# One decoder layer on one core: the causal mask moved into VectorE's maximum, compressed keys stored by residue modulo 8, and a rewritten order of steps

## The chip, the core and the metric

The kernel runs on one core of one Trainium2 chip. The core has five engines that run side by side: TensorE (PE in the rows; PEld is its weight load), VectorE (DVE), ScalarE (ACT), GpSimd (POOL) and SyncE (SP), which here only issues DMA transfers. The metric is the device time of one execution in microseconds, lower being better; a time is the median of three runs.

## The reference, cut to what matters

One layer of a decoder works on 512 tokens of width 1024. A modulated normalisation feeds one input projection, whose columns feed two groups of heads; their outputs are concatenated and projected, and a gated MLP with a short convolution follows. The change touches the sparse attention of eight query heads with two groups of keys:

```python
q = rope_partial(rmsnorm(to_heads(q_pre, NSA_HEADS, hd), q_g), pos)
k_c = rope_partial(rmsnorm(to_heads(kc_pre, G, hd), k_g[0]), pos)
...
cidx = np.arange(n_cmp)[:, None] * 16 + np.arange(32)[None]        # 31 overlapping blocks of 32 tokens
flat = (k_c[:, :, cidx] + pe).reshape(B, G, n_cmp, 32 * 64)
k_cmp = silu(flat @ w1) @ w2                                       # the same for v_cmp
...
sc = jnp.where(kpos <= t, q @ k.T * scale, NEG)                    # selected and window branch
p = softmax(sc); o = p @ v
```

With 512 tokens the selected branch keeps all of its eight blocks and the window covers all earlier tokens, so that both branches are causal attention over all earlier keys, with keys and values of their own.

## The kernel before

All tokens lie in four tiles of 128. The program has three stages. First the modulation's first columns, the normalised input and the projections of the queries and of one gate are worked out (to about 57 us). Then comes a stage in which everything else of the first sub-layer is interleaved by hand (to about 275 us). Then the output projection, the up-projection and the down-projection follow; they are long rows of matmuls with 512 columns.

Products of float32 quality are made from two rounded parts each (`split`, lines 139 to 141: ScalarE makes the high part, VectorE the rest; `mm3`, lines 143 to 146: three matmuls). Weights come through two buffers `raw`: `take` issues the load of the next weights when the present ones are taken, `piece` splits a half of them one use ahead. SyncE issues all loads in program order, each when its buffer has been read.

The middle stage is seven Python generators. The strings of `ORDER` say, letter by letter, which one emits its next step; each engine executes its instructions in the order in which they are emitted and waits only for data and buffers. In this document d46 is the step of the 47th letter `d`, counted from 0.

- `d`: dense work. d0 to d15 are the projection of keys and values, d16 to d23 the projection for the compressed branch, d24 to d39 two projections of the recurrent heads, d40 is `cmp_flat` (it forms the blocks with their position sums), and `cmp_hidden` multiplies them by `w_cmp1` in four quarters: d46, d48, d58 and d60 hold the matmuls (line 888). d53 to d56 and d61 to d64 project values; d65 to d72 project and turn others, the first turning being emitted in d69 and the second in d73 (line 1253).
- `p`: squares, roots, rope (`norm`, lines 689 to 704) and turning of queries, keys and compressed inputs.
- `a`: attention. A unit is a tile, a head and one or two branches: tiles 0 and 1 take both branches in one unit (16 units), tiles 2 and 3 one branch (32 units). An even `a` step emits the scores and their maximum, the following odd one the exponential.
- `c`: `cmp_out` in four steps; c0 applies the activation to what d60 has summed, c1 turns it, c2 multiplies by `w_cmp2`.
- `s`: sums of the modulation on VectorE (line 1333), one load of 512 KB each.
- `l`, `m`: levels of the recurrence of two pairs of heads.

For the mask, units of tiles 0 and 1 add it on TensorE, by a matmul of an identity with the mask (line 981), and VectorE takes one maximum over both branches (line 982); the exponential reads PSUM. Units of tiles 2 and 3 do it in one VectorE instruction that adds the mask, takes the maximum and writes the masked scores to SBUF (line 978).

For the compressed branch, a tile's keys and values are written twice side by side for each group, turned by four transposes (line 838), and copied so that even tokens lie in the lower 64 partitions and odd ones in the upper (lines 841, 842). d40 adds the positions in eight instructions that read every eighth element, four on VectorE and four on GpSimd (line 875).

Of the kernel before, what the change touches and what calls it, by code (L numbers as in the profile page):

```python
# [19 lines left out]
P = 128  # L20
# [35 lines left out]
ORDER = ("pddpddpppspddppddsdppspdpddpddpppddpsdpdddddpdpddpdpdddddppaspddaapaddaspapsaddaddsdalpppapaadlddlld",  # L56
         "aadadadsladasaladlldaadlddallladdddslaalllddsaaalddcddcsamcllmcdaaamlaadaaldmsadaadamaaaaamamsdlaala",
         "daadlammdalmaadmamaldsaaadmmmlaammaadlmmlasmdalaaaaamadaadaaddasadamdmmsadmllalaaaasmmammaalmaadamsl",
         "aadldddmmaasasldaadaaamlaaadmmladmaaaasamamdaaaamldds")
# [40 lines left out]
def hybrid_layer_kernel(ctx: ExitStack, tc: tile.TileContext, d: dict, out: bass.AP, dbg=None):  # L100
# [353 lines left out]
    identb = cst.tile([P, P], BF16, name="identb")  # L454
    causb = cst.tile([P, P], BF16, name="causb")
# [6 lines left out]
    def gate_tables():  # L462
        gp.tensor_copy(identb, ident)
# [225 lines left out]
    def norm(n):  # L689
# [5 lines left out]
        for hf in range(2):  # L695
            ve.tensor_tensor(rt[:, :, :, 8 * hf:8 * hf + 8], xr[:, :, :, 8 - 8 * hf:16 - 8 * hf],
                             st[:, :, 8 * hf:8 * hf + 8].unsqueeze(2).to_broadcast([P, t, g, 8]), ALU.mult)
# [6 lines left out]
        n.append(dst)  # L704

    def prep(steps):

        for step in steps:
            for f, u in [(w[0], w[1:]) for w in step.split()]:
                if f == "s":  # L710
                    units[u] = squares(makers[u[0]](int(u[1])))
                elif f == "r":
                    root(units[u])
                elif f == "n":
                    norm(units[u])
                elif f == "f":
                    units[u][0][4](units[u])
                else:
                    units[u][0][5](units.pop(u))
            yield  # L720
# [5 lines left out]
    def hg_forget(pr, j, a):  # L726
# [8 lines left out]
        ve.tensor_scalar(k[:, :, ::1 - 2 * j], t3, fc2n[:, h:h + 1], fc2[:, h:h + 1], ALU.mult, ALU.add)  # L735

    def hg_query(pr, j, a):
# [4 lines left out]
        ve.scalar_tensor_tensor(HG[pr][2][:, j], th, 1.0, a, ALU.add, ALU.mult)  # L742

# [63 lines left out]
    kv2 = G([2, 2, 256], s="kv2")  # L807
# [14 lines left out]
    def a_unit(i):  # L822
        def copy_vg(n):
# [3 lines left out]
            vd = TMP([P, 2, 2, HD], tag="vd")  # L827
            sc.copy(vd, acca[i][:, P:2 * P].rearrange("p (g e) -> p g e", e=HD).unsqueeze(2)
                    .to_broadcast([P, 2, 2, HD]))
            n.append(vd)  # L830

        def flip_kv(n):
            ps = PS()
            for b in range(2):
                for g in range(2):
                    q = b * 2 + g
                    src = n[3][:, g] if b else n[2][:, 0, g]
                    pe.transpose(ps[:, q * P:(q + 1) * P], src.rearrange("p a e -> p (a e)"), ident)
            pv = ps.rearrange("p (q u two) -> p q u two", q=4, two=2)
            kv = kv2.rearrange("p b g u -> p (b g) u")  # L840
            sc.copy(kv[0:64, :, i * 64:(i + 1) * 64], pv[0:64, :, :, 0])
            sc.copy(kv[64:128, :, i * 64:(i + 1) * 64], pv[64:128, :, :, 1])

        return (acca[i][:, 0:P].rearrange("p (a g e) -> p a g e", a=1, e=HD), stab[:, i:i + 1, 1],
                ctab[:, i:i + 1, 1], 2, copy_vg, flip_kv)
# [19 lines left out]
    def cmp_flat():  # L865
        ps = PS()
        pe.transpose(ps[:, 0:32], perow, ident[0:32, 0:32])
        ve.tensor_copy(pet, ps[:, 0:32])
        for b in range(2):
            f = G([16, 2, 32], s="flat")  # L870
            gp.memset(f[:, :, :, 31:32], 0.0)
            for g in range(2):
                for m2 in range(2):
                    src = kv2[:, b, g, 8 * m2:8 * m2 + 248].rearrange("p (n m) -> p m n", m=8)
                    (gp if g else ve).tensor_tensor(f[:, 8 * m2:8 * m2 + 8, g, 0:31], src,
                                                    pet[:, b * 16 + 8 * m2:b * 16 + 8 * m2 + 8].unsqueeze(2)
                                                    .to_broadcast([P, 8, 31]), ALU.add)
# [4 lines left out]
    def cmp_hidden(mq):  # L882
        w1 = take(f"w1{mq}")
        yield
        for m in range(4):
            for b in range(2):
                mm = 4 * mq + m
                pe.matmul(cps[0][64 * b:64 * b + 64, 0:256], FL[b][:, mm].rearrange("p g n -> p (g n)"),
                          w1[:, b, m], start=(mm == 0), stop=(mm == 15))
        yield  # L890

    def cmp_out():
        cth = TMP([P, 256], tag="cth")
# [26 lines left out]
        for g in range(2):  # L920
            ve.tensor_tensor(BD[:, g], ps[:, 64 + g * HD:64 + (g + 1) * HD].unsqueeze(1).to_broadcast([P, 4, HD]),
                             cb[:, C_BLK:C_BLK + 4].unsqueeze(2).to_broadcast([P, 4, HD]), ALU.mult)
        yield
# [17 lines left out]
    def cmp_scores(i):  # L941
        ps = PS("S")
# [22 lines left out]
    def scores(u):  # L965
        i, h, bs = u
        if h is None:
            return cmp_scores(i)
        g, W, n = h // 4, (i + 1) * P, len(bs)
# [4 lines left out]
        pe.matmul(o, QS[i][:, h], KK[g, 1][:, 0:i + 1, bsl], start=False, stop=(n == 1))  # L974
        mx = SM([P, 2], "mx")
        if n == 1:
            pt = TMP([P, 512], tag="pt")
            ve.tensor_tensor_reduce(pt[:, 0:W], ps[:, 0:W], cmask[:, 512 - W:512], -1.0, 1e30, ALU.add, ALU.min,
                                    mx[:, 0:1])
            return pt, mx  # L980
        pe.matmul(o[:, i], identb, causb.unsqueeze(1).to_broadcast([P, n, P]), start=False, stop=True)
        ve.tensor_reduce(mx[:, 0:n], ps[:, 0:n * W].rearrange("p (b w) -> p b w", b=n), AX.X, ALU.max,
                         negate=True)
        return ps, mx

    def expo(u, st):
# [4 lines left out]
        ps, mx = st  # L991
        W, n = (i + 1) * P, len(bs)
        pt = ps if n == 1 else TMP([P, 512], tag="pt")
# [3 lines left out]
        for e in range(n):  # L997
            sl = slice(e * W, (e + 1) * W)
            sc.activation(pt[:, sl], ps[:, sl], AF.Exp, bias=mx[:, e:e + 1], scale=(-1.0 if n == 1 else 1.0),
# [736 lines left out]
```

## Time and profile before

| what | value |
|---|---|
| median of three runs | 699.4 us (698.62 to 699.52) |
| the profiled execution | 699.39 us |
| its span, from first to last instruction | 697.6 us |
| busy share of PE, DVE, ACT, POOL | 98%, 65%, 47%, 17% |
| granted clock of TensorE | full in all 40 slices |

The profile comes from one execution, whose own time is that of the median; 1.8 us of it lie outside the span. Busy time of TensorE is modelled with a tail that overlaps the next matmul, so it is better to read the starts of its instructions: the distance between two starts is what an instruction costs when nothing waits.

### The profile page before, as it was taken

The page shows a single profiled execution, that of the slowest core. Times are in us where ns is not written, and L with a number is a line of the kernel's source. Part 1 is how long each engine was busy: PE and PEld are TensorE (multiplying, and loading weights), DVE is VectorE, ACT ScalarE, POOL GpSimd, SP SyncE. Part 2 cuts the span into 40 slices and gives each one's busy share as a digit, 9 for nine tenths or more (in the row PEclk, how much of TensorE's full clock was granted, in tenths as well). Part 3 has the DMA queues.
Part 4 walks back from the last instruction along what each step waited for, and adds up shares of the span by engine and source line. Part 5 has one row for each costly group of instructions (what it writes and reads, how often), then busy time and mean ns, then how long its engine had stood idle before and what let it go on. Part 6 is the DMA issues. An engine that isn't in the chain of part 4 may idle for free.

```text
span 697.6 us, 10902 instructions
## 1 busy us (share of the span) xinstructions
PE 687.0 (98%) x4263; PEld 566.5 (81%) x4264; DVE 453.2 (65%) x882; ACT 326.0 (47%) x624; POOL 117.5 (17%) x119
## 2 busy tenths in 40 slices
PE   8999999999999999999999999999999999999997
PEld 4678898787887879888988888888888888888886
DVE  5588989968889879688656666655555554225224
ACT  5564446665676778245444443344433443111210
POOL 2005022200020200100047437511011010000000
PEclk9999999999999999999999999999999999999999
DMA  9996443568213226162053454523424323124301
GB/s 284 295 291 196 124 148 97 187 205 272 92 33 121 62 62 214 59 178 69 12 163 117 132 152 122 150 71 110 121 61 120 96 86 122 62 101 170 120 31 60
DMA packets 100487, 90.16 MB, mean 129 GB/s; under 512 B 5787, under 2 KB 83539, under 8 KB 100437
## 3 DMA queue, kind: packets, MB, share of 16 engines
q1 hardware_dynamic: 100181, 89.38, 42.0%
q8 instruction: 33, 0.54, 0.3%
q10 hardware_dynamic: 256, 0.11, 0.1%
q14 instruction: 17, 0.14, 0.1%
HBM read 87.37 MB, written 2.11 MB: 128 GB/s over the span
## 4 chain that ended last, share of the span: by engine, by line
PE 77%; DVE 10%; ACT 5%; DMA 4%; SPq 2%; issue 1%; POOL 0%; ACTq 0%; DVEq 0%
PE u L146 11%; PE u L144 11%; PE u L145 11%; PE dn L144 6%; PE dn L145 6%; PE dn L146 6%; PE pT L144 2%; PE pT L146 2%; PE pT L145 2%; PE oT L1059 2%; PE F L1031 2%; PE oh L144 2%; PE oh L146 2%; PE oh L145 2%; DMA raw<-in_w_in 1%; DVE rows L399 1%
## 5 line engine op out<-in xcount | busy, mean ns | idle before, releaser
L141 DVE TENSOR_TENSOR wlo<-raw,whi 128x1024 fp32r<-128x1024 f32 (+1 forms) x87 | 111.3, 1280 | 136.1 <-ACT whi L140 135.5
L140 ACT CAST whi<-raw 128x1024 fp32r<-128x1024 f32 (+1 forms) x87 | 89.8, 1032 | 102.3 <-PE dn L146 80.1
L144 PE MATMUL u<-h2h,whi 128*128 128x512 f32 (+1 forms) x360 | 136.7, 380 | 0.0
L145 PE MATMUL u<-h2l,whi 128*128 128x512 f32 (+1 forms) x360 | 136.7, 380 | 0.0
L146 PE MATMUL u<-h2h,wlo 128*128 128x512 f32 (+1 forms) x360 | 136.6, 380 | 0.0
L145 PEld LDWEIGHTS u<-h2l,whi 128*128 128x128 f32 x360 | 67.7, 188 | 12.9
L146 PEld LDWEIGHTS u<-h2h,wlo 128*128 128x128 f32 x360 | 67.7, 188 | 12.8
L144 PEld LDWEIGHTS u<-h2h,whi 128*128 128x128 f32 x360 | 67.7, 188 | 12.7
L145 PE MATMUL dn<-wlo,gT 128*128 128x512 f32 (+1 forms) x160 | 62.1, 388 | 0.0
L146 PE MATMUL dn<-whi,gT 128*128 128x512 f32 (+1 forms) x160 | 62.1, 388 | 0.0
L144 PE MATMUL dn<-whi,gT 128*128 128x512 f32 (+1 forms) x160 | 62.0, 388 | 0.0
L1623 POOL TENSOR_TENSOR y<-y,y 128x512 f32<-128x512 f32 x22 | 28.4, 1290 | 165.7 <-DVE y L1618 165.7
L140 ACT CAST gT<-y 128x512 fp32r<-128x512 f32 x20 | 12.4, 622 | 71.2 <-POOL y L1623 71.2
L141 DVE TENSOR_TENSOR gT<-y,gT 128x512 fp32r<-128x512 f32 x20 | 14.8, 742 | 42.7 <-ACT gT L140 42.7
L144 PE MATMUL pT<-hT,whi 128*128 128x512 f32 x96 | 39.2, 409 | 0.0
L146 PE MATMUL pT<-hT,wlo 128*128 128x512 f32 x96 | 37.7, 393 | 0.0
L145 PE MATMUL pT<-hT,whi 128*128 128x512 f32 x96 | 37.5, 391 | 0.0
L1621 ACT ACTIVATE y<-y 128x512 f32<-128x512 f32 x22 | 13.9, 632 | 49.6 <-DVE y L1618 49.6
L145 PEld LDWEIGHTS dn<-wlo,gT 128*128 128x128 f32 x160 | 30.0, 188 | 6.4 <-DVE wlo L141 0.2
L144 PEld LDWEIGHTS dn<-whi,gT 128*128 128x128 f32 x160 | 30.0, 188 | 6.2
L146 PEld LDWEIGHTS dn<-whi,gT 128*128 128x128 f32 x160 | 30.0, 188 | 6.2
L1616 ACT ACTIVATE y<-u,cv 128x512 f32<-128x512 f32 x44 | 33.9, 772 | 0.0
(378 smaller groups left out, 1410.2 us busy)
## 6 DMA issues: line engine op xcount, KB each, us to landing
raw<-in_w_up SPq DMA_DIRECT2D x44, 512.0 KB, 4.2
aw<-in_w_ada SPq DMA_DIRECT2D x24, 512.0 KB, 4.0
raw<-in_w_down SPq DMA_DIRECT2D x10, 1024.0 KB, 5.1
ada<-in_w_ada SPq DMA_DIRECT2D x32, 256.0 KB, 5.7
raw<-in_w_in SPq DMA_DIRECT2D x7, 1024.0 KB, 6.6
x<-in_x SPq DMA_DIRECT2D x8, 512.0 KB, 4.8
raw<-in_w_cmp SPq DMA_DIRECT2D x8, 512.0 KB, 5.6
raw<-in_w_out SPq DMA_DIRECT2D x4, 1024.0 KB, 6.1
```

Of the source, the lines that this page charges most:

```text
L140: sc.copy(hi, src)
L141: (eng or ve).tensor_tensor(lo, src, f32(hi), ALU.subtract)
L144: pe.matmul(o, ah, bh, start=start, stop=False, skip_group_check=True)
L145: pe.matmul(o, ah, bl, start=False, stop=False, skip_group_check=True)
L146: pe.matmul(o, al, bh, start=False, stop=stop, skip_group_check=True)
L399: ve.scalar_tensor_tensor(t, w, cs[:, j:j + 1], t, ALU.mult, ALU.add)
L1031: pe.transpose(ps[:, j * P:(j + 1) * P], src[:, j * P:(j + 1) * P], ident)
L1059: pe.matmul(oTs[i][r:r + 64, h // 2], VV[:, j, b, g], src[:, q * P:(q + 1) * P], start=(h == 0 and b == 0 and j == 0), stop=False, skip_gr ...
L1616: sc.activation(y, u, AF.Identity, bias=cv[:, 132 + c:133 + c], scale=cv[:, 88 + c:89 + c])
L1621: sc.activation(y, y, AF.Silu)
L1623: gp.tensor_tensor(ys[0], ys[0], y, ALU.mult)
```

## The change

- The mask of tiles 0 and 1 is added as in tiles 2 and 3: one VectorE instruction for each branch adds it, takes the maximum and writes to SBUF. The mask matmul, its two constant tiles and the maximum over both branches go.
- Compressed keys and values are no longer doubled: two transposes for a tile instead of four, and four smaller copies instead of two, which sort the tokens by their residue modulo 8. The position sums read neighbouring elements, in four VectorE instructions over both groups; GpSimd takes no part.
- The rope's product of swapped halves is one instruction for each tile and projection, with the halves read in reversed order, instead of two.
- `ORDER` has the same 353 letters, with the same count of each, in another sequence.

The lines that only add to a set `there` or assert on it while the program is built are left out.

```diff
-ORDER = ("pddpddpppspddppddsdppspdpddpddpppddpsdpdddddpdpddpdpdddddppaspddaapaddaspapsaddaddsdalpppapaadlddlld",
-         "aadadadsladasaladlldaadlddallladdddslaalllddsaaalddcddcsamcllmcdaaamlaadaaldmsadaadamaaaaamamsdlaala",
-         "daadlammdalmaadmamaldsaaadmmmlaammaadlmmlasmdalaaaaamadaadaaddasadamdmmsadmllalaaaasmmammaalmaadamsl",
-         "aadldddmmaasasldaadaaamlaaadmmladmaaaasamamdaaaamldds")
+ORDER = ("dppddpsdppddppppdppdddpsdsdppdpdpdpddpsddpddddpddpddpdddppadpsddaapdaappaapdsddsdddaapapadaaddsdddaa",
+         "dsldaallaallaadllaapdlldsdddddladlasldslddlaalldcmcaacalascdddmllaaaalamddldaaaadmaasamaaamlamsdaama",
+         "ddaaladmlammamsdmaalmalmdadaamlamamamadaadaasllaammasdadadsaaaalmasdamadlamadaamldaammlasmlmadaammma",
+         "mlalddddlmsaalasmaadamaaadaaadlaasmaaasmdddaamaaadlma")
...
         rt = TMP([P, t, g, 16], tag="rt")
-        for hf in range(2):
-            ve.tensor_tensor(rt[:, :, :, 8 * hf:8 * hf + 8], xr[:, :, :, 8 - 8 * hf:16 - 8 * hf],
-                             st[:, :, 8 * hf:8 * hf + 8].unsqueeze(2).to_broadcast([P, t, g, 8]), ALU.mult)
+        for a in range(t):
+            ve.tensor_tensor(rt[:, a].rearrange("p g (two e) -> p g two e", two=2),
+                             xr[:, a, :, 0:16].rearrange("p g (two e) -> p g two e", two=2)[:, :, ::-1],
+                             st[:, a].rearrange("p (two e) -> p two e", two=2).unsqueeze(1)
+                             .to_broadcast([P, g, 2, 8]), ALU.mult)
...
-    kv2 = G([2, 2, 256], s="kv2")
+    kv2 = G([2, 2, 8, 32], s="kv2")
...
-            vd = TMP([P, 2, 2, HD], tag="vd")
-            sc.copy(vd, acca[i][:, P:2 * P].rearrange("p (g e) -> p g e", e=HD).unsqueeze(2)
-                    .to_broadcast([P, 2, 2, HD]))
+            vd = TMP([P, P], tag="vd")
+            sc.copy(vd, acca[i][:, P:2 * P])
...
-            for b in range(2):
-                for g in range(2):
-                    q = b * 2 + g
-                    src = n[3][:, g] if b else n[2][:, 0, g]
-                    pe.transpose(ps[:, q * P:(q + 1) * P], src.rearrange("p a e -> p (a e)"), ident)
-            pv = ps.rearrange("p (q u two) -> p q u two", q=4, two=2)
-            kv = kv2.rearrange("p b g u -> p (b g) u")
-            sc.copy(kv[0:64, :, i * 64:(i + 1) * 64], pv[0:64, :, :, 0])
-            sc.copy(kv[64:128, :, i * 64:(i + 1) * 64], pv[64:128, :, :, 1])
+            for b, src in enumerate((n[2].rearrange("p t g a e -> p (t g a e)"), n[3])):
+                pe.transpose(ps[:, b * P:(b + 1) * P], src, ident)
+            pv = ps[:, 0:256].rearrange("p (b u two) -> p b u two", b=2, two=2)
+            for g in range(2):
+                for r in range(2):
+                    sc.copy(kv2[64 * r:64 * r + 64, :, g, :, 8 * i:8 * i + 8],
+                            pv[64 * g:64 * g + 64, :, :, r].rearrange("p b (n m) -> p b m n", m=8))
...
-                ctab[:, i:i + 1, 1], 2, copy_vg, flip_kv)
+                ctab[:, i:i + 1, 1], 1, copy_vg, flip_kv)
...
-            for g in range(2):
-                for m2 in range(2):
-                    src = kv2[:, b, g, 8 * m2:8 * m2 + 248].rearrange("p (n m) -> p m n", m=8)
-                    (gp if g else ve).tensor_tensor(f[:, 8 * m2:8 * m2 + 8, g, 0:31], src,
-                                                    pet[:, b * 16 + 8 * m2:b * 16 + 8 * m2 + 8].unsqueeze(2)
-                                                    .to_broadcast([P, 8, 31]), ALU.add)
+            for m2 in range(2):
+                ve.tensor_tensor(f[:, 8 * m2:8 * m2 + 8, :, 0:31],
+                                 kv2[:, b, :, :, m2:m2 + 31].rearrange("p g m n -> p m g n"),
+                                 pet[:, b * 16 + 8 * m2:b * 16 + 8 * m2 + 8].unsqueeze(2).unsqueeze(3)
+                                 .to_broadcast([P, 8, 2, 31]), ALU.add)
...
-        pe.matmul(o, QS[i][:, h], KK[g, 1][:, 0:i + 1, bsl], start=False, stop=(n == 1))
+        pe.matmul(o, QS[i][:, h], KK[g, 1][:, 0:i + 1, bsl], start=False, stop=True)
         mx = SM([P, 2], "mx")
-        if n == 1:
-            pt = TMP([P, 512], tag="pt")
-            ve.tensor_tensor_reduce(pt[:, 0:W], ps[:, 0:W], cmask[:, 512 - W:512], -1.0, 1e30, ALU.add, ALU.min,
-                                    mx[:, 0:1])
-            return pt, mx
-        pe.matmul(o[:, i], identb, causb.unsqueeze(1).to_broadcast([P, n, P]), start=False, stop=True)
-        ve.tensor_reduce(mx[:, 0:n], ps[:, 0:n * W].rearrange("p (b w) -> p b w", b=n), AX.X, ALU.max,
-                         negate=True)
-        return ps, mx
+        pt = TMP([P, 512], tag="pt")
+        for e in range(n):
+            ve.tensor_tensor_reduce(pt[:, e * W:(e + 1) * W], ps[:, e * W:(e + 1) * W], cmask[:, 512 - W:512], -1.0,
+                                    1e30, ALU.add, ALU.min, mx[:, e:e + 1])
+        return pt, mx
...
-            sc.activation(pt[:, sl], ps[:, sl], AF.Exp, bias=mx[:, e:e + 1], scale=(-1.0 if n == 1 else 1.0),
+            sc.activation(pt[:, sl], pt[:, sl], AF.Exp, bias=mx[:, e:e + 1], scale=-1.0,
```

## Rows read from the trace of the kernel before

**Rows 1.** The page's line of busy time, share of the span and instructions of each engine.

```profile
PE 687.0 (98%) x4263; PEld 566.5 (81%) x4264; DVE 453.2 (65%) x882; ACT 326.0 (47%) x624; POOL 117.5 (17%) x119
```

**Rows 2.** Busy time in three stretches: the interleaved stage, ten microseconds within it, and the up-projection. Columns: stretch, its length, then busy time and instructions of PE, PEld, DVE, ACT and POOL, the granted clock, the DMA engines' share, GB/s.

```profile
57.00:275.00 218.00, 215.43 (x1983) 180.08 (x1982) 186.65 (x468) 139.61 (x341) 30.75 (x44) 1.00 0.43 138
...
125.00:135.00 10.00, 10.00 (x118) 8.20 (x120) 9.83 (x18) 5.69 (x18) 4.17 (x5) 1.00 0.35 124
...
340.00:570.00 230.00, 230.00 (x1056) 192.16 (x1055) 132.53 (x151) 99.22 (x134) 73.07 (x54) 1.00 0.39 114
```

**Rows 3.** TensorE's instructions in order of time, at a mask matmul (L981) and at the transposes of compressed values (L838). Columns: start, duration, engine, line, operation, tiles, shape, count.

```profile
133.69 0.28 PE L981 MATMUL S<-causb,identb 128*128 128x256 bf16 x1
133.81 0.38 PE L1031 MATMUL F<-cb,pt 128*128 128x128 f32 x2
...
125.97 0.38 PE L838 MATMUL ps<-cb,vd 128*128 128x128 f32 x2
126.19 0.38 PE L1031 MATMUL F<-cb,pt 128*128 128x128 f32 x2
```

**Rows 4.** TensorE's groups of instructions by line and shape in the interleaved stage: count, busy us, mean ns of one, idle time before them.

```profile
L981 PE MATMUL S<-causb,identb 128*128 128x256 bf16 x16 | 4.5, 283 | 0.0
...
L838 PE MATMUL ps<-cb,dst 128*128 128x128 f32 x8 | 1.6, 280 | 0.0
...
L838 PE MATMUL ps<-cb,vd 128*128 128x128 f32 x8 | 1.5, 273 | 0.0
```

**Rows 5.** TensorE's instructions in order of time, the four of the interleaved stage with the longest idle time before them; the idle time and what ended it stand in brackets.

```profile
81.96 0.66 PE L751 MATMUL ps<-cb,dst 128*128 128x128 f32 x4 [0.48 <-DVE dst L702]
...
163.06 1.94 PE L888 MATMUL cps<-raw,flat 128*64 128x256 f32 x14 [0.41 <-DMA raw<-in_w_cmp]
...
207.26 0.65 PE L1253 MATMUL ps<-cb,hvT 128*128 128x128 f32 x4 [0.56 <-ACT hvT L1244]
...
248.69 0.69 PE L1133 MATMUL lev<-hgQ,hgE 128*64 128x64 f32 x16 [0.67 <-ACT pT L1038]
```

**Rows 6.** VectorE's instructions in order of time: the maximum of a unit of tile 0 (L982, 256 columns) and of tile 1 (512) with what starts after each, and the masked maximum (L978) of 384 and of 512 columns with the reading of its accumulator.

```profile
138.52 0.42 DVE L982 TENSOR_REDUCE mx<-S 128x2 f32<-128x256 f32 x1
138.85 0.75 DVE L1335 TENSOR_SCALAR aacc<-aw,cs 128x1024 f32<-128x1024 f32 x1
139.51 0.68 DVE L982 TENSOR_REDUCE mx<-S 128x2 f32<-128x512 f32 x1
140.11 0.17 DVE L1014 RECIPROCAL su<-su 128x4 f32<-128x4 f32 x1
...
186.29 0.55 DVE L978 CUSTOM_DVE_ANT_0 pt<-S,cmask 128x384 f32<-128x384 f32 x1
186.77 0.08 DVE L978 DVE_READ_ACCUMULATOR2_ANT mx<- 128x1 f32 x1
...
248.58 0.69 DVE L978 CUSTOM_DVE_ANT_0 pt<-S,cmask 128x512 f32<-128x512 f32 x1
249.19 0.08 DVE L978 DVE_READ_ACCUMULATOR2_ANT mx<- 128x1 f32 x1
```

**Rows 7.** The position sums of line 875: engine, operation, count, then least, median and greatest duration of one in ns, first and last start, shape.

```profile
L875 DVE TENSOR_TENSOR flat<-kv,pet x4: 643/1064/1098, 129.2 to 131.8; 128x248 f32<-128x248 f32 x4
L875 POOL TENSOR_TENSOR flat<-kv,pet x4: 964/1057/1202, 129.2 to 132.4; 128x248 f32<-128x248 f32 x4
```

**Rows 8.** VectorE's four position sums and its next instruction in order of time, and TensorE's first matmuls on their result.

```profile
129.21 3.63 DVE L875 TENSOR_TENSOR flat<-kv,pet 128x248 f32<-128x248 f32 x4
132.76 0.41 DVE L1162 TENSOR_TENSOR hgA<-lev,cb 128x256 f32<-128x256 f32 x1
...
134.12 1.95 PE L888 MATMUL cps<-raw,flat 128*64 128x256 f32 x16
```

**Rows 9.** VectorE's instructions in order of time in the rope of the last queries: the two products of swapped halves, and an addition of 128 columns.

```profile
80.61 0.36 DVE L696 TENSOR_TENSOR rt<-xr,stab 128x64 f32<-128x64 f32 x2
...
81.61 0.29 DVE L702 TENSOR_TENSOR dst<-dst,rt 128x128 f32<-128x128 f32 x1
```

**Rows 10.** ScalarE's exponentials by shape in the interleaved stage: from SBUF with 384 columns, from PSUM with 256. Columns as in rows 4.

```profile
L999 ACT ACTIVATE pt<-pt,mx 128x384 f32<-128x384 f32 x16 | 9.9, 620 | 7.5 <-DVE mx L978 5.2 <-DVE hgtot L1202 1.4 <-DVE su L1014 0.8
...
L999 ACT ACTIVATE pt<-S,mx 128x256 f32<-128x256 f32 x16 | 7.5, 472 | 6.6 <-DVE mx L982 6.6
```

**Rows 11.** All engines in order of time around the compressed keys: TensorE's first matmul behind d60, VectorE's step of c0, and TensorE's m0 (L1122) and c2 (L912).

```profile
164.93 0.39 PE L144 MATMUL pt<-whi,hT 128*128 128x256 f32 x1
...
165.46 0.42 DVE L896 SCALAR_TENSOR_TENSOR chs<-cth,cps 128x256 f32<-128x256 f32 x1 [1.08 <-ACT cth L894]
...
168.65 0.86 PE L1122 MATMUL lev<-hgQ,hgK 128*32 128x32 f32 x64
169.44 0.66 PE L912 MATMUL ps<-chT,wpe 128*128 128x64 f32 x4
```

**Rows 12.** ScalarE, VectorE and SyncE in order of time: the split of the two halves of the value weights, and the issue of the load of the last quarter of `w_cmp1` that this frees a buffer for.

```profile
146.29 1.05 ACT L140 CAST whi<-raw 128x1024 fp32r<-128x1024 f32 x1 [1.49 <-DMA raw<-in_w_in]
...
156.35 1.23 DVE L141 TENSOR_TENSOR wlo<-raw,whi 128x1024 fp32r<-128x1024 f32 x1 [1.60 <-ACT whi L140]
...
157.60 0.92 SPq L207 DMA_DIRECT2D raw<-in_w_cmp  x2
```

More of the change, by code (lines that the diff above doesn't have):

```diff
@@ L453, in hybrid_layer_kernel @@
     onesr = cst.tile([P, P], F32R, name="onesr")
-    identb = cst.tile([P, P], BF16, name="identb")
-    causb = cst.tile([P, P], BF16, name="causb")
     bsc2 = cst.tile([P, 8], F32, name="bsc2")
@@ L462, in gate_tables @@
     def gate_tables():
-        gp.tensor_copy(identb, ident)
         sc.copy(identr, ident)
@@ L704, in norm @@
         n.append(dst)
+    there = set()
     def prep(steps):
@@ L717, in prep @@
                     units[u][0][4](units[u])
+                    there.add(f + u)
                 else:
                     units[u][0][5](units.pop(u))
+                    there.add(f + u)
             yield
@@ L735, in hg_forget @@
         ve.tensor_scalar(k[:, :, ::1 - 2 * j], t3, fc2n[:, h:h + 1], fc2[:, h:h + 1], ALU.mult, ALU.add)
+        there.add(("f", pr, j))
     def hg_query(pr, j, a):
@@ L742, in hg_query @@
         ve.scalar_tensor_tensor(HG[pr][2][:, j], th, 1.0, a, ALU.add, ALU.mult)
+        there.add(("q", pr, j))
     QS = []
@@ L865, in cmp_flat @@
     def cmp_flat():
+        assert all(f"la{j}" in there for j in range(NT))
         ps = PS()
@@ L889, in cmp_hidden @@
                           w1[:, b, m], start=(mm == 0), stop=(mm == 15))
+        if mq == 3:
+            there.add("hidden")
         yield
     def cmp_out():
+        assert "hidden" in there
         cth = TMP([P, 256], tag="cth")
@@ L922, in cmp_out @@
                              cb[:, C_BLK:C_BLK + 4].unsqueeze(2).to_broadcast([P, 4, HD]), ALU.mult)
+        there.add("compressed")
         yield
@@ L941, in cmp_scores @@
     def cmp_scores(i):
+        assert "compressed" in there
         ps = PS("S")
@@ L968, in scores @@
             return cmp_scores(i)
+        assert all(f"lk{j}" in there for j in range(i + 1))
         g, W, n = h // 4, (i + 1) * P, len(bs)
@@ L990, in expo @@
             return st
-        ps, mx = st
+        pt, mx = st
         W, n = (i + 1) * P, len(bs)
-        pt = ps if n == 1 else TMP([P, 512], tag="pt")
         if h % 2 == 0:
@@ L1011, in weigh @@
         pt, su = st
+        assert f"fa{i}" in there
         W, n = (i + 1) * P, len(bs)
@@ L1054, in values @@
         g = h // 4
+        assert all(f"fk{j}" in there for j in range(i + 1))
         for e, b in enumerate(bs):
@@ L1154, in hg_levels @@
     def hg_levels(pr, res):
+        assert all((f, pr, j) in there for f in "fq" for j in range(2))
         TT, KS, QP = HG[pr]
@@ L1217, in hg_levels @@
         S = G([2, 3, P], s="hgS")
+        assert "even values" in there and "odd values" in there
         for j in range(2):
@@ L1236, in hg_value_out @@
         sc.copy(HV[0][:, 2 * hb:2 * hb + 2], a.rearrange("p (i c) -> p i c", i=2))
+        if hb:
+            there.add("even values")
     def hg_value_odd():
@@ L1254, in flip_out @@
             sc.copy(HV[1][:, :, h * P:(h + 1) * P], ps.rearrange("p (i c) -> p i c", i=NT))
+            if h:
+                there.add("odd values")
         for _ in proj_T(out):
@@ L1458, in part @@
             yield
-    gp.tensor_copy(causb, cb[:, C_CAUS:C_CAUS + P])
     gp.memset(cmask[:, 0:384], 0.0)
```

## The prediction

> **What bounds the kernel now.** I read the busy line first: TensorE is busy for 98% of the span, no other engine for more than two thirds [rows 1]. Since its busy time is modelled, I looked at stretches next. In the up-projection 1056 matmuls of 512 columns take 230 us, 0.218 us each, back to back [rows 2]; nothing of the change lies there. The interleaved stage is the one to study: TensorE idles for 2.57 of 218 us (218.00 less 215.43), VectorE for 31, ScalarE for 78 [rows 2]. So TensorE sets the end of this stage too, and an instruction taken from it counts in full, while one moved to VectorE costs nothing unless a result comes later than TensorE asks for it. VectorE can be that late: between 125 and 135 us it works 9.83 of 10 us [rows 2]. Third, I read what ended TensorE's idle times. Four make up 2.12 of the 2.57 us: for a query's rope on VectorE, for a load, and two for ScalarE [rows 5]. The reordering can remove or add waits of this kind.
>
> **TensorE's work that goes.** A mask matmul costs the distance to the next start, 133.81 less 133.69 = 0.12 us [rows 3]; its 0.28 us of duration overlap the next. There are 16 [rows 4], so 1.92 us. Two transposes take 126.19 less 125.97 = 0.22 us [rows 3], so 0.11 each; 16 are now made [rows 4] and eight stay, so 0.88 us. Together 2.80 us, with little doubt: both groups have no idle time before them [rows 4], so they hide no wait.
>
> **VectorE's masked maximum.** The masked maximum of 384 columns occupies VectorE for 186.77 less 186.29 = 0.48 us, that of 512 for 0.61, and the reading of the accumulator starts together with what follows [rows 6]. That is 0.13 us for 128 columns, so 0.35 for 256 and 0.22 for 128 (estimates from these rows). A unit of tile 0 needs two of 128, 0.44 us, where it needed 0.33; one of tile 1 two of 256, 0.70, where it needed 0.60 [rows 6]. Sixteen units: 1.7 us more. If whole durations counted instead of distances (0.55 and 0.69, hence 0.41 and 0.27, with 0.08 for each reading), it would be some 6 us; the starts show that they don't, so I take 1.7. The exponentials now read SBUF. 384 columns cost 0.62 us there, 256 in PSUM 0.47 [rows 10], so one of 256 gets dearer by at most 0.15, 4.8 us over the 32; ScalarE's 78 us of idle time cover it. The four smaller copies for two in each tile are covered in the same way; without that cover both would delay the transposes of the unit four units later.
>
> **Position sums.** Eight adds of 248 columns ran on two engines at once. VectorE's four occupy it from 129.21 to 132.76, 3.55 us [rows 8], one lasting 643 ns and the others 1.04 to 1.10 us while GpSimd's took as long [rows 7]. Four adds of 496 columns now run on VectorE alone. The nearest row by size is the 512-column maximum, 0.61 us [rows 6], so 2.4 us. From the other side, if 248 columns keep their median of 1.064 us [rows 7], an add takes 2.13 and the four 8.5 us. I take 2.4, since both reasons to be slow that the rows show are gone: elements eight apart, and a second engine at the same memory. On this the Trainium skill has two rules. In "SBUF — State Buffer", section "Who interferes with whom", a VectorE instruction with two SBUF inputs contends with a GpSimd instruction that reads SBUF; 1.04 us beside GpSimd against 643 ns agrees, though no row shows the add without it. [...]
>
> **Rope.** Two products take 0.36 us; one of double width about 0.29, as the addition of 128 columns [rows 9]. That is 0.07 us for each of four query tiles, 0.28 in all before the turning that waited 0.48 us [rows 5], because VectorE works without a pause there. Compressed tiles save as much again, and half the width of two more instructions; key tiles keep two products. In sum VectorE has about as much to do as before: 1.7 more for the masks, 1.1 less for the adds, 0.6 or more less for the rope.
>
> **The order.** I compared the sequences at the four idle places. (1) The rope: the same work stands ahead of it, so the 0.28 us of VectorE come off the wait (bounds 0 and 0.48). (2) The load for d60 was issued when the split of the value weights' second half had ended at 157.59, and TensorE went on at 163.06, 5.46 us after the issue at 157.60 [rows 5, 12]. That split, issued in d53, stood behind a22, l9, l10, l11 and a23; it now follows d52 directly, so a maximum (0.60) and three level steps of VectorE no longer delay it, while only a27, a28 and the empty l16 leave the stretch up to d60. I count 0.41 off (bounds 0 and 0.41). SyncE's queue has the modulation load of s11 behind this one, and nobody needs that one soon. (3) d73's turning waited 0.56 us [rows 5]; between it and d72 a55 and m13 now stand as well, three transposes (0.33) and 32 small products (half of m0's 169.44 less 168.65 = 0.79, [rows 11]). I count 0.45 off. (4) The large products of m29 waited 0.67 us [rows 5]; d84, six matmuls of 0.218 = 1.3 us, now stands ahead of them. I count 0.60 off. Together 1.74 us.
>
> One place gets worse. Behind d60 ScalarE and VectorE must apply the activation before c1 can turn it: TensorE passed d60 at 164.93, VectorE was done at 165.46 + 0.42 = 165.88, 0.95 us later [rows 11]. d61 and d62, 24 matmuls, covered this; now m0 alone does, 0.79 us. So c1 waits at least 0.16 us, longer where VectorE is behind. c2 needs five VectorE instructions behind c1, and a27 and a28 stand between them instead of s12, a29 and m0. Queued behind both on TensorE is everything. I take 0.7 us for both; the bounds are 0.16 and two hand-overs uncovered in full, 1.9 us. For the rest of the 353 steps, each shifted by a few places, I add 0.4 us; the bounds are 0.45 less (the idle time not listed) and 2.6 more (as much idle time as the stage now has).
>
> **Sum.** -1.92 - 0.88 - 1.74 + 0.7 + 0.4 = -3.4 us. The profiled execution took 699.39 us (a span of 697.6 and 1.8 us around it), the median is 699.4: 696.0 us. About 0.2%, 1.4 us, is what a measurement of this kernel can tell from no change.
>
> **The rivals.** *All waits go*: TensorE loses its 2.80 us, the idle 2.57 disappear and c1 costs next to nothing: 694.0. For it speaks that three of four idle places get more cover; against it, that 353 moved steps seldom leave none.
>
> *No change*: TensorE arrives earlier, and what it waits for doesn't. The value weights' landing held ScalarE at 146.29, for 1.49 us [rows 12]; their load queues behind others on SyncE. If it comes no earlier, TensorE, ahead by some 2.4 us there, gives back up to 1.5, and with c1 and c2 at their upper bound of 1.9 all is gone: 699.4.
>
> *Slower, by the position sums alone*: d46's first matmuls need three of the four adds. They started at 134.12 [rows 8]; without eight masks, the transposes and 0.28 of the first wait, and with l0 (0.79) and a15 (0.3) now behind them, TensorE gets there at about 130.9. The adds began at 129.21, and with s7 now behind them at about 128.0. So an add may take 0.97 us before it is felt. At 2.13 us the third ends at 134.4, 3.5 us late; the load of the next quarter, issued behind the fourth add and a split, makes d48 late by some 1.7 more: 701.2. For it speaks VectorE's 9.83 of 10 us and the 1.064 us of rows 7; against it, that the elements are now neighbours and GpSimd is out of the way. [...]
>
> **How the numbers follow.** The forecast has a chance of 0.50, all waits gone 0.20, no change 0.19, slower 0.11. The predicted time is the forecast's, 696.0 us. The range leaves the slower case out and reaches to the other two, 693.3 to 699.4 us; the forecast's own, with the bounds of c1 and c2 and of the rest, is 694.6 to 697.9. So faster has 0.70, no difference 0.19, slower 0.11.
>
> **What would show it.** No L981, eight L838 on TensorE; 64 masked maxima, 0.22 and 0.35 us apart for the narrow ones; adds near 0.6 us, and d46 with no idle time before it; no idle time for the load of d60; up to 1 us of it before L900 and L912; TensorE's idle time in the stage near 2 us. The prediction is wrong if that idle time grows by 3 us or more, or if the adds take over 1 us.

## The result, and the profile after

The changed kernel takes **693.5 us** (693.4 to 694.3), the kernel before 699.25 us beside it: a ratio of 0.9922, interval 0.9905 to 0.9939. Faster by 5.7 us, as forecast in sign; the forecast was 3.4 us. The time is inside the range, 0.2 us above its lower end, and below the forecast's own 694.6 to 697.9 us.

The page's busy line after, which answers to [rows 1], and the interleaved stage of both kernels, from the first product of d0 to the first instruction behind the last step (columns as in [rows 2]; the kernel before first):

```profile
PE 682.5 (99%) x4240; PEld 564.3 (81%) x4240; DVE 452.5 (65%) x922; ACT 327.1 (47%) x632; POOL 112.9 (16%) x113
```

```profile
60.88:275.69 214.81, 212.24 (x1972) 177.58 (x1971) 185.11 (x463) 136.90 (x338) 26.87 (x36) 1.00 0.42 134
```

```profile
61.55:270.57 209.02, 207.25 (x1948) 175.08 (x1947) 184.29 (x501) 138.22 (x346) 22.20 (x32) 1.00 0.44 138
```

The difference lies in this stage: 209.02 for 214.81 us, 5.8 less. Behind it both kernels take 418.4 us. The profiled execution of the changed kernel is only 5.1 us shorter as a whole (694.30 for 699.39), since its stage begins 0.67 us later, at 61.55 for 60.88; over the 14 profiled executions here that start lies between 60.04 and 61.55. TensorE executes 24 instructions fewer (1948 for 1972), and VectorE, with 38 more, is no busier. TensorE's idle time went only from 2.57 to 1.77 us. So 5.0 of the 5.8 us are "busy" time that is gone, and 24 instructions account for 2.8 of it. Where the rest came from is what the experiments had to tell.

VectorE's position sums and TensorE's first matmuls on them, after (answering to [rows 8]):

```profile
128.92 2.43 DVE L876 TENSOR_TENSOR flat<-kv,pet 128x496 f32<-128x496 f32 x4
...
131.42 1.95 PE L890 MATMUL cps<-raw,flat 128*64 128x256 f32 x16
```

Four adds in 2.35 us (the next instruction starts at 131.27) are 0.59 us for each, and d46 starts without idle time. The masked maxima of a unit of tile 0, after (answering to [rows 6]), start 0.21 us apart:

```profile
131.27 0.28 DVE L986 CUSTOM_DVE_ANT_0 pt<-S,cmask 128x128 f32<-128x128 f32 x1
131.48 0.09 DVE L986 DVE_READ_ACCUMULATOR2_ANT mx<- 128x1 f32 x1
131.48 0.29 DVE L986 CUSTOM_DVE_ANT_0 pt<-S,cmask 128x128 f32<-128x128 f32 x1
```

The places where TensorE still waits, answering to [rows 5] and, for c1, [rows 11]:

```profile
81.77 0.39 PE L146 MATMUL kva<-whi,hT 128*128 128x512 f32 x1
82.49 0.66 PE L756 MATMUL ps<-cb,dst 128*128 128x128 f32 x4 [0.33 <-DVE dst L701]
...
135.46 0.41 PE L1035 MATMUL F<-cb,pt 128*128 128x128 f32 x2 [0.47 <-DVE pt L1026]
...
158.80 1.95 PE L890 MATMUL cps<-raw,flat 128*64 128x256 f32 x16
...
161.69 0.44 PE L905 MATMUL ps<-cb,chs 128*128 128x128 f32 x2 [0.16 <-DVE chs L901]
...
191.86 0.66 PE L1262 MATMUL ps<-cb,hvT 128*128 128x128 f32 x4 [0.22 <-ACT hvT L1253]
...
240.00 0.63 PE L1035 MATMUL F<-cb,pt 128*128 128x128 f32 x4 [0.40 <-ACT pt L1002]
```

d60 (158.80) no longer waits for its load. The waits at p15 and at a turning of value tiles are shorter, the one before m29's products is gone, and two new ones stand at 135.46 and 240.00. The first two lines show how to read an idle time. Products of this shape start 0.23 us apart, so L756 should have started at 82.00 and not at 82.49: the wait cost 0.49 us, though only 0.33 is shown as idle. The end of the last matmul ahead of a wait is modelled, and hides about 0.16 us of it.

### The profile page after: what moved, and what is told of

Same layout as the page of the kernel before. It is cut to its first block, busy times and chain, and to the rows that moved or that the text cites. A ratio compares the mean times of both kernels' runs of the same rounds, so it can differ in the third digit from the quotient of the medians.

```text
span 692.5 us, 10891 instructions
## 1 busy us (share of the span) xinstructions
PE 682.5 (99%) x4240; PEld 564.3 (81%) x4240; DVE 452.5 (65%) x922; ACT 327.1 (47%) x632; POOL 112.9 (16%) x113
## 4 chain that ended last, share of the span: by engine, by line
PE 78%; DVE 12%; ACT 4%; DMA 2%; SPq 2%; issue 1%; ACTq 0%; DVEq 0%
PE u L144 12%; PE u L145 12%; PE u L146 12%; PE dn L145 6%; PE dn L146 6%; PE dn L144 6%; PE oh L144 2%; PE oh L146 2%; PE oh L145 2%; PE oT L1064 2%; PE F L1035 2%; DVE wlo L141 2%; PE pT L146 2%; PE pT L144 2%; PE pT L145 2%; DVE rows L399 1%
## 5 line engine op out<-in xcount | busy, mean ns | idle before, releaser
L1002 ACT ACTIVATE pt<-pt,mx 128x128 f32<-128x128 f32 (+3 forms) x64 | 36.0, 564 | 9.4 <-DVE mx L986 8.3
```

The lines of the kernel that those rows point to most:

```text
L1002: sc.activation(pt[:, sl], pt[:, sl], AF.Exp, bias=mx[:, e:e + 1], scale=-1.0, accum_out=su[:, h % 2, e:e + 1])
```

## The experiments

All medians are of several runs, each beside the kernel before on the same chip. The stage is that of the profiled execution, bounded as above. What a step costs "by the starts" is the sum of the distances from each of its starts on TensorE to the next start there, so that a wait counts for the step in front of it.

| kernel | median us | to before, us | ratio, interval | stage us |
|---|---|---|---|---|
| before | 699.25 | | | 214.8 |
| e3 masks alone, old order | 699.53 | +0.5 | 0.9998 to 1.0015 | 214.9 |
| e4 keys alone, old order | 697.19 | -1.8 | 0.9963 to 0.9984 | 213.3 |
| e1 all new code, old order | 697.58 | -1.5 | 0.9971 to 0.9988 | 213.3 |
| e2 old code, new order | 697.70 | -1.3 | 0.9972 to 0.9990 | 213.3 |
| e11 as e1, one step moved | 696.19 | -2.9 | 0.9945 to 0.9970 | 212.2 |
| e6 after, old masks | 696.24 | -3.0 | 0.9942 to 0.9969 | 212.0 |
| e7 after, old keys | 694.65 | -4.6 | 0.9922 to 0.9947 | 210.5 |
| e5 after, old rope | 693.89 | -5.2 | 0.9911 to 0.9938 | 209.5 |
| e9 after, half the sums on GpSimd | 693.78 | -5.4 | 0.9906 to 0.9934 | 209.3 |
| after | 693.53 | -5.7 | 0.9905 to 0.9939 | 209.0 |
| e12 after, ScalarE reads PSUM | 694.80 | -4.0 | 0.9928 to 0.9955 | 210.3 |
| e8 after, six places moved | 698.59 | -0.6 | 0.9980 to 0.9998 | 214.0 |
| e10 after, four places moved | 692.42 | -6.6 | 0.9891 to 0.9919 | 208.3 |

**Code against order (e1, e2).** In e1 the string `ORDER` of the kernel before stands in the kernel after, in e2 the other way round.

> All the new code, with the 353 steps in the order of before. Theory A, the two halves add up: 24 instructions fewer on TensorE count in full in any order (16 masks by 0.12 and 8 transposes by 0.11 us, 2.8 us), and the order is worth what is left of the 5.8 us that the stage lost, so this order gives 699.3 - 2.8 = about 696.5 us (696.1 to 696.9). Rival B, the new code pays only in the order that was made for it, because in the old one VectorE's added work comes late for somebody: 698 to 700 us. Rival C, the stalls went because VectorE and GpSimd were freed by the code and not because of the order: 693.5 to 694.3 us.

> The old code (masks as products of TensorE, sixteen transposes, GpSimd's half of the position sums) with the steps in the new order. Theory A: the order alone is worth about 3.0 us, 696.3 us (695.8 to 696.8). Rival B: the new order without the new code gains little, 698 to 700 us, for then GpSimd's adds of 1.06 us stand ahead of the hidden products again. Rival C: 699.3 us, no change.

697.6 and 697.7 us: alone, the code is worth 1.5 us and the order 1.3, together 5.7. Theory A, the halves add up, falls; so does C. B is right that each half alone gains little, but both times lie below its 698 us. Some 2.9 us exist only when both are there. The next four runs look for them.

**The masks alone (e3).** The two constant tiles go too, and the exponential reads the masked scores from SBUF, as in the changed kernel.

```diff
-        pe.matmul(o[:, i], identb, causb..., start=False, stop=True)
-        ve.tensor_reduce(mx[:, 0:n], ..., AX.X, ALU.max, negate=True)
+        for e in range(n):
+            ve.tensor_tensor_reduce(pt[:, e * W:(e + 1) * W], ps[:, ...], cmask[:, 512 - W:512], ...)
```

> Kernel before with one edit, the masks of all tiles in VectorE's maximum, old order. Theory A: 16 products of 0.12 us less, 697.4 us (697.1 to 697.7). Rival: the scores' maxima come later (0.22 and 0.35 us for 0.16 and 0.28), and the flips wait for it, so that less than half of it arrives: 698.4 us or more.

699.5 us: sixteen instructions fewer, and nothing gained. TensorE's rows of e3, then its busy time and granted clock there (columns as in [rows 2]):

```profile
135.45 0.40 PE L971 MATMUL S<-KK,qs 128*128 128x512 f32 x1
137.28 0.71 PE L1023 MATMUL F<-cb,pt 128*128 128x128 f32 x2 [1.44 <-DVE pt L1014]
137.93 0.84 PE L1340 MATMUL rows<-aacc,ones 128*32 128x256 f32 x8
138.70 1.98 PE L1051 MATMUL oT<-pT,VV 128*64 128x128 f32 x16
```

```profile
135.85:137.28 1.43, 0.00 (x0) 0.00 (x0) 1.36 (x9) 0.83 (x5) 0.00 (x0) 1.00 0.27 80
137.28:137.93 0.65, 0.59 (x3) 0.28 (x3) 0.15 (x1) 0.65 (x4) 0.00 (x0) 1.00 1.07 381
137.93:138.70 0.77, 0.77 (x10) 0.16 (x9) 0.28 (x1) 0.71 (x2) 0.00 (x0) 0.70 1.09 383
138.70:140.60 1.90, 1.90 (x20) 1.57 (x16) 1.90 (x9) 1.16 (x6) 0.00 (x0) 0.50 1.10 387
```

The same two places in the kernel before:

```profile
137.16 0.33 PE L1031 MATMUL F<-cb,pt 128*128 128x128 f32 x1 [0.19 <-ACT pt L1020]
137.99 1.09 PE L1059 MATMUL oT<-pT,VV 128*64 128x128 f32 x16
```

VectorE, busy without a pause from 125.75 to 137.42 us, is later by the masks' own work while TensorE is earlier: a16 costs 1.48 us more by its starts. And after this wait of 1.44 us the granted clock falls from 1.00 to 0.50, from 2.4 to 1.2 GHz. The sixteen small products of a18 take 1.98 us for 1.09, and a18 costs 1.42 more. Against these 2.9 us stand some 1.9 for the masks and 1.05 at d60, which TensorE now reaches after its load. The rival, that the flips wait, was right; the clock nobody had expected.

**The keys alone (e4).** `cmp_flat` and the compressed branch of `prep` as after, all else as before.

> Kernel before with one edit, the compressed keys turned once and the position sums in four adds of 496 columns on VectorE, old order. Theory A: 8 transposes of 0.11 us less, 698.4 us (698.1 to 698.7), the sums hidden or nearly. Rival: in the old order the four adds (2.4 us in a row on VectorE) end after the matmul that reads them wants them, and it costs what it gains: 699.2 us or more. A second rival: narrow products ahead of wide ones cost the wide one about 0.09 us, and 7 such places go with the transposes: 697.8 us.

697.2 us, outside all three ranges: more came than the transposes' 0.88 us. By the starts of the steps a17 gained 0.41 us (the sums occupy VectorE for 2.35 us, from 128.15 to 130.50, and not for 3.55) and d60 0.49. Its load is issued when VectorE has split weights, so an earlier VectorE is also an earlier load: 4.89 us ahead of d60's first product (155.00 and 159.89), 4.41 in the kernel before (157.60 and 162.01). The last rival's wide products got no shorter.

**The parts undone in the new order (e6, e7, e5).** Each is the changed kernel with one part as it was.

> The changed kernel with one part undone: the masks of tiles 0 and 1 are products of TensorE again (16 of 0.12 us), everything else and the order as changed. Theory A, VectorE is as late as TensorE between 110 and 140 us, and the masks paid nothing in the old order only because the long position sums (3.6 us) held VectorE's queue there; with the short sums they pay in full: 695.4 us (695.0 to 695.8). Rival B, the masks pay nothing in any order, since what they take from TensorE they give to VectorE in the same stretch: 693.3 to 693.9 us.

> The changed kernel with one part undone: compressed keys with sixteen transposes and the position sums in eight strided adds on two engines again. Theory A: the parts don't add up, the long sums bring back both their own cost (1.8 us by the run of the keys alone) and the wait that ate the masks' gain (1.9 us): 697.0 us (696.5 to 697.6). Rival B, parts add up: 693.5 + 1.8 = 695.3 us.

> The changed kernel with one part undone, the rope's products in halves of the rotated columns again. Theory A, VectorE's time counts only where TensorE waits for it, and of the rope's places that is p15 alone (0.33 us of idle time before L756 at 82.49): its wait grows by 0.28, 693.8 us (693.6 to 694.1). Rival B: the rope's instructions stand in VectorE's full queue between 78 and 117 us, and all that they got shorter comes back: 694.5 to 695.5 us.

Without the masks 696.2 us: worth nothing in the old order, they are worth 2.7 us here, more than their 1.9 and more than either theory has. Without the keys 694.7: worth 1.1 us, less than alone, since the half microsecond at d60 is there without them; the wait at 135.46 grew by 0.48 us, a quarter of what Theory A wanted back; the time lies below both theories. Without the rope 693.9, as Theory A had it. By its time alone it can't be told from the changed kernel; by the starts d13, whose last product p15 waits behind, is 0.28 us longer. What the masks gave beyond their own time is this line of e6:

```profile
115.88 0.39 PE L983 MATMUL S<-KK,qs 128*128 128x256 f32 x1 [0.87 <-DVE hgQ L749]
```

Scores wait 0.87 us at a place where the changed kernel waits for nothing, and p27, the step in front of it, costs 1.12 us more; e2, the other kernel with old masks and new order, has the same wait (0.71 us at 117.43).

**Who holds the scores' tile (e12).** The masked maximum leaves VectorE as the only reader of the scores in PSUM; before, ScalarE read them there too, later.

```diff
-        return pt, mx
+        return pt, mx, ps if n == 2 else pt
...
-            sc.activation(pt[:, sl], pt[:, sl], AF.Exp, bias=mx[:, e:e + 1], scale=-1.0,
+            sc.activation(pt[:, sl], ps[:, sl], AF.Tanh if n == 2 else AF.Exp, bias=mx[:, e:e + 1],
+                          scale=(1.0 if n == 2 else -1.0),
```

> The changed kernel, VectorE masking as changed, but in tiles 0 and 1 ScalarE reads the scores from PSUM, where they stand unmasked, and not VectorE's masked copy; so that the numbers stay finite it takes the hyperbolic tangent of them and not the exponential, and the output is not the reference's. The number, width and order of the instructions stay. Theory A: with the old masks in the new order a matmul of scores at 115.88 us waited 0.87 us for VectorE's reading of a projection, because a PSUM tile of scores that ScalarE reads is let go later than one that only VectorE's maximum reads, and the next scores then take over a tile still in use. The wait comes back here without any mask on TensorE: 694.6 us (694.3 to 694.9). Rival B, that wait is due to the work on TensorE or VectorE that the old masks bring: 693.2 to 693.7 us.

694.8 us, and the wait is back with no mask on TensorE. First TensorE, then ScalarE's last reading of the scores before:

```profile
115.36 0.38 PE L981 MATMUL S<-KK,qs 128*128 128x256 f32 x1 [1.14 <-ACT pt L1002]
...
114.83 0.39 ACT L1002 ACTIVATE pt<-S,mx 128x128 f32<-128x128 f32 x1
```

It ends when ScalarE has done reading the scores before. So Theory A holds: with the maximum as the last reader, a PSUM tile comes free earlier, and in the new order that is worth 1.3 us. The intervals of the two ratios overlap a little; by the starts the steps say the same, with 1.39 us more at p27, 0.38 more at a28 and 0.64 less at a16. The tile that is still in use is not the same one as in e6, though. As the programs are built, the scores that wait (step a6) take over the PSUM bank of a projection in e6 and e2, which VectorE reads last, and the bank of a0's scores here and in the changed kernel. So e12 shows what the later reading costs at this place; it is not a copy of e6's wait.

**The load of d60 (e11).**

```diff
 # ORDER of before, new code
-  d52 a22 l9 l10 l11 a23 d53
+  d52 d53 a22 l9 l10 l11 a23
```

> All the new code in the order of before with one step moved, d53 (the split of the value weights' second half, which frees the buffer for the load that d60 waits for) ahead of a22, l9, l10, l11 and a23. Theory A, in the old order what the masks take from TensorE is given back at d60, whose load comes when VectorE has done that split, and not when TensorE asks (idle 1.14 us at d60 there, 1.48 us by the starts): without the wait 696.1 us (695.8 to 696.5). Rival B: the split waits for the landing of its own load (ScalarE before it, VectorE 1.76 us idle), so its place in the order changes nothing: 697.4 to 697.8 us.

First d60 in e1, then in e11:

```profile
159.86 0.65 PE L890 MATMUL cps<-raw,flat 128*64 128x256 f32 x2 [0.30 <-DMA raw<-in_w_cmp]
161.34 1.94 PE L890 MATMUL cps<-raw,flat 128*64 128x256 f32 x14 [0.84 <-DMA raw<-in_w_cmp]
```

```profile
159.63 1.95 PE L890 MATMUL cps<-raw,flat 128*64 128x256 f32 x16
```

One step moved gives 1.4 us (696.2), as Theory A had it. The load's issue moved from 155.88 us in e1 to 151.82 in e11; in the changed kernel it is at 150.23, in [rows 12] at 157.60.

```profile
155.88 0.92 SPq L207 DMA_DIRECT2D raw<-in_w_cmp  x2
```

```profile
150.23 0.93 SPq L207 DMA_DIRECT2D raw<-in_w_cmp  x2
```

Not all of this belongs to the 2.9 us that exist only when both halves are there, for the order alone removes the wait too: in e2 the products of d60 start at 162.05 and m0 behind them at 163.93, without a wait. What belongs to the 2.9 is that the wait is longer in e1 than in the kernel before, 1.48 for 1.05 us at d60 and 0.37 more at a28 in front of it: of what the code takes from TensorE in the old order, 0.8 us are spent there.

By the starts, the interplay (after less e1, less e2, plus before) is 2.70 us: 0.95 at p27, 0.62 at a28, 0.43 at d60, 0.29 at d18, and the rest spread over many steps. The first three, 2.0 us, are places that e12 and e11 change; d18 has no run of its own.

**Half the sums on GpSimd (e9).**

```diff
-            for m2 in range(2):
-                ve.tensor_tensor(f[:, 8 * m2:8 * m2 + 8, :, 0:31], ...)
+            for g in range(2):
+                for m2 in range(2):
+                    (gp if g else ve).tensor_tensor(f[:, 8 * m2:8 * m2 + 8, g, 0:31], kv2[:, b, g, :, m2:m2 + 31], ...)
```

> The changed kernel with the position sums in the new layout, but halved again: four adds of 248 columns on VectorE, four on GpSimd. Theory A: GpSimd's four take about 1.06 us each as before, end near 133.2 us instead of VectorE's 131.4, and the hidden products d46 wait: 694.3 to 695.3 us. Rival B: VectorE's half falls to 0.33 us each, its queue is 1.1 us shorter, and the wait of the flips at 135.46 us goes: 692.7 to 693.2 us.

```profile
L877 DVE TENSOR_TENSOR flat<-kv,pet x4: 418/814/819, 128.4 to 130.2; 128x248 f32<-128x248 f32 x4
L877 POOL TENSOR_TENSOR flat<-kv,pet x4: 718/774/838, 128.4 to 130.7; 128x248 f32<-128x248 f32 x4
```

693.8 us, no difference to the changed kernel; both theories fall. GpSimd is quicker than [rows 7] had it (0.77 for 1.06 us with neighbouring elements), so d46 does not wait. But VectorE gains nothing by giving half away: its four adds of 248 columns occupy it from 128.40 to 130.95, 2.55 us, four of 496 without GpSimd from 128.92 to 131.27, 2.35 us. The first, which starts 0.04 us ahead of GpSimd's first, takes 418 ns, the other three some 815. This agrees with the rule of the Trainium skill ("SBUF — State Buffer", "Who interferes with whom") that the prediction went by, and speaks against handing these adds on.

**Six and four places of the order (e8, e10).** Both move steps where the changed kernel still waits.

```diff
 # e8
-  d13 p15 d14 p16
+  d13 d14 p15 p16
-  s7 d43 d44 d45 a13 a14
+  d43 d44 d45 a13 s7 a14
-  c0 m0 c1 a27 a28
+  c0 m0 a27 c1 a28
-  m6 s14 d68 a47
+  s14 d68 m6 a47
-  l30 a81 m23 a82 d82
+  a81 a82 l30 m23 d82
-  d92 d93 d94 a110 a111 m38
+  d92 a110 a111 d93 d94 m38
```

```diff
 # e10 (and the fourth and the last of e8's)
-  s2 d11 p12 p13
+  d11 p12 s2 p13
-  l32 a87 s20 m27 l33 m28 a88 d84
+  l32 d84 a87 s20 m27 l33 m28 a88
```

> The changed kernel with six places of the order changed, each where the trace after shows TensorE waiting: p15 behind d14, the modulation sum s7 behind a13, a27 ahead of c1, m6 behind d68, l30 behind a82, d93 behind a111. Theory A, a stall costs what the starts of TensorE's instructions show (0.49 + 0.3 + 0.34 + 0.39 + 0.58 + 0.32 = 2.4 us): 691.1 us (690.8 to 691.6). Rival B, a stall costs the idle time that the profile shows there (0.33 + 0.2 + 0.16 + 0.22 + 0.40 + 0.1 = 1.4 us): 692.1 us (691.8 to 692.4). Rival C, the waits come back at the next instruction of the same queue: 693.2 to 693.8 us.

> The changed kernel with four places of the order changed, none of which moves a modulation sum ahead of or behind VectorE's work between 125 and 145 us: the sum s2 behind p12, m6 behind d68, d84 ahead of a87, d93 behind a111. Theory A, each wait that the trace after shows there goes by the distance between starts (0.49, 0.2, 0.5 and 0.17 us): 692.2 us (691.9 to 692.6). Rival B: as with the six swaps, something that was covered before is late instead: 693.3 us or more.

e8 gave nearly the whole gain back, 698.6 us, far above all three theories. VectorE's row there, then TensorE's, then the granted clock (line numbers are greater by one):

```profile
138.96 0.75 DVE L1347 TENSOR_SCALAR aacc<-aw,cs 128x1024 f32<-128x1024 f32 x1 [3.71 <-DMA aw<-in_w_ada]
```

```profile
140.54 0.48 PE L982 MATMUL S<-KK,qs 128*128 128x512 f32 x1 [3.03 <-DVE mx L987]
140.85 0.60 PE L983 MATMUL S<-KK,qs 128*128 128x512 f32 x1
141.38 3.36 PE L891 MATMUL cps<-raw,flat 128*64 128x256 f32 x16
```

```profile
141.38:144.00 2.62, 2.62 (x14) 1.48 (x15) 2.55 (x14) 1.76 (x7) 0.00 (x0) 0.50 0.77 193
```

The step s7 doesn't only sum. It also issues the load that s8 needs. Moved behind a13 it comes, on SyncE, behind a load of `w_cmp1` that waited for VectorE until 132.25; the modulation load went out at 133.33 and not at some 122 to 126 us (the two loads that the changed kernel issues from 122.25 on). s8, unmoved, held VectorE's queue for 3.71 us, the scores' maxima stood behind it, and TensorE waited 3.03 us. The clock fell again: d48 took 3.29 us for 1.88. By the starts a19, where the wait is, and d48 cost 4.7 us more, about as much as the whole run lost; s7 was not moved back alone. e10 has no such place and took 692.4 us, 1.1 less than the changed kernel, though the intervals of the two ratios overlap. By starts p15's wait gave 0.49 us there, for the 0.33 that the profile shows as idle, and the one at a87 0.47 for 0.40; d20 gave 0.40 back. So Theory A's measure holds where nothing else moves, and by its median e10 is the fastest of all.

## Why the prediction was right, and where it was mis-sized

**TensorE's instructions (-2.80): right here, wrong as a rule.** Sixteen masks and eight transposes are gone; by starts most units lost 0.12 us each (12 of 16 in e3, where the order is that of before), the turning of a compressed tile 0.22. But "an instruction taken from it counts in full" does not hold in every order: with the old one e3 shows the masks' 1.9 us lost entirely, while the transposes' 0.88 came in full (e4).

**The masked maxima (no cost): right in size, incomplete.** 128 columns start 0.21 us apart, 256 columns 0.34, where 0.22 and 0.35 were estimated. The prediction saw that the exponentials now read SBUF and counted only their time; that a PSUM tile comes free earlier, worth 1.3 us (e12), is missing from it. Its proviso, that a result can come later than TensorE asks for it, is what happens in the old order: a16 costs 0.58 us more in e1 and 1.48 in e3.

**Position sums (hidden, 2.4 us): right.** 2.43 us, 0.67 for one, no wait at d46. The slower rival needed 2.13 us for one. The Trainium skill ("Perfetto Trace Analysis", "Optimizing Scalar/DVE Operations") says that offloading some work of a saturated VectorE, even to GpSimd, may make sense, and adds that the two share an SBUF read port, so that between them it might not help; e9, with 2.55 us of VectorE beside GpSimd for 2.35 without it, agrees with what it adds.

**The rope (-0.28): right.** p15's wait, 0.48 us in [rows 5], is 0.33 now, and e5 gives the 0.28 back.

**Four waits (-1.74): mechanisms right, size wrong.** By starts the four steps in which [rows 5] waited lost 1.05 us (d60), 0.73 (before m29's products), 0.72 and 0.63, together 3.1 us, where the prediction took 1.74 out of 2.12 us of idle time. The term was read from the idle column, and this column leaves out the modelled tail of the matmul in front. Two waits were not removed but moved: p15 to the end of d13 (0.49 back) and the turning from d73 to d69 (0.38 back).

**c1 and c2 (+0.7): too high.** c1 waits 0.16 us, the lower bound; m0 is 0.23 longer by starts, c2 0.20 shorter. a27 and a28 cover what VectorE does behind c1.

**The rest of the steps (+0.4): wrong sign.** The stage's 5.79 us less 2.80 for the instructions and 2.26 for the four waits (3.13 less what moved) leave 0.73; with the 0.09 that m0, c1 and c2 cost together, the other steps lost some 0.8 us. New waits cost 1.19 of these steps: 0.49 before 135.46, 0.47 before 240.00, 0.23 at d20. Against them a17, d18 and a61 lost 0.38, 0.30 and 0.26, and many dense steps about 0.1 each.

So the time is nearest to the rival in which all waits go (694.0), yet not for its reason: 1.77 us of idle time remain. That it lies in the range at all is owed to the range's reaching to this rival; the forecast's own missed it by 1.1 us. Of the 2.3 us that the forecast of 3.4 lacks, 0.5 are in the waits (2.26 for 1.74), 0.6 in c1 and c2, and 1.2 in the rest of the steps. And the no-change rival's mechanism is real: TensorE arrives earlier at a load that gains less. That is what e1 does (d60 is reached 2.15 us earlier than before, its load issued 1.72 us earlier), and the new order's early d53 is what prevents it, as point (2) of the prediction said.

Two sums of the prediction do not come out of its terms. With c1 and c2 at 1.9 and the rest at 2.6 us the forecast's own upper end is 699.4 and not 697.9 us; and the no-change rival counts the 0.7 us of c1 and c2 twice, without which it gives 698.7. The measured time touches neither.

What stays open: the 0.29 us of the interplay at d18 and the some 0.4 that lie in no single step, and why d20 is late again in e10.

## What to carry to other kernels

Price a wait by the distance between starts against that of undisturbed instructions of the same shape; the idle column here left out 0.06 to 0.64 us of each. Before an instruction is taken from the busiest engine, look for the next thing that has its own clock (a load, another engine's queue): there the gain can be spent (e3), and a change of order can bring it out. And when a step is moved, move with open eyes every load that it issues: here one step cost nearly 5 us by a load that nobody was thinking of.

## What the runs showed of the hardware

The granted clock of TensorE fell from 2.4 to 1.2 GHz behind a wait of 1.44 us (e3) and one of 3.03 us (e8), and stood at 0.50 from 138.70 to 140.60 (e3) and from 141.38 to 144.00 (e8); behind waits of 0.87 (e6), 1.14 (e12) and twice in short order 0.30 and 0.84 us (e1) it stayed at 1.00. The lower clock cost 0.9 us in e3's small products alone, so that this wait cost about twice what it shows (1.48 us at a16 and 1.42 at a18). And of VectorE's adds of two SBUF tiles beside GpSimd's, those behind the first take 815 ns and not 418 (e9): two engines together (done at 131.5 us, begun at 128.4) are no faster than one (131.3, begun at 128.9).
